# Rows of 64 KB instead of 32 KB for the loads and stores of a grouped instance norm

## Chip, cores, metric

The kernel runs on one core of a Trainium2 chip. The metric is the time of one execution on the device in microseconds (us), as a median of repeated runs. Runs over 1.5% above the fastest of the same kernel count as slow and are left out of ratios. Each kernel is compared with runs of the kernel before on the same chip in the same session.

## The reference, cut to what matters

```python
# x: (4, 8, 16, 256, 256) float32, gamma: (8, 16)
mu    = x.mean(axis=(3, 4), keepdims=True)          # over 65536 values of one channel
var   = ((x - mu) ** 2).mean(axis=(3, 4), keepdims=True)
out   = (x - mu) / np.sqrt(var + 1e-5) * gamma[None, :, :, None, None]
```

There are 512 channels of 256 KB each, so 134.2 MB come in and 134.2 MB go out. Nothing can be stored before its whole channel has been read.

## The kernel before

A unit is 16 channels of 65536 values. It lies on 128 partitions, each with an eighth of a channel: 8192 float32, one *row* of 32 KB. A unit moves as one DMA of 128 rows. Six slots take turns; slot `u % 6` is loaded, summed, normalised in place and stored, and then loaded again.

```python
    S = 8;  K = P // S;  F = HW // S        # 8 partitions a channel, rows of 8192 float32 = 32 KB
    U = n_ch // K                           # 32 units
    AHEAD = 6
    xv = x....rearrange("(u p f) -> u p f", p=P, f=F)
    slots = [data.tile([P, F], F32, name=f"xt{i}") for i in range(AHEAD)]
    def load(u, queue):
        queue.dma_start(out=slots[u % AHEAD][:], in_=xv[u])
    # ... first six loads, constants (cut) ...
    for u in range(U):
        t = slots[u % AHEAD]
        nc.vector.reduce_sum(out=st[:, u, 0:1], in_=t[:], axis=AX.X)                 # L103
        nc.scalar.activation(out=junk[:], in_=t[:], func=ACTF.Square, accum_out=st[:, u, 1:2])  # L104
        # ... matmul over the 8 partitions of a channel, 1/std, scale (cut) ...
        nc.vector.tensor_scalar(out=t[:], in0=t[:], scalar1=ps[:, 0:1], scalar2=scale[:, u:u+1],
                                op0=ALU.add, op1=ALU.mult)                           # L126
        nc.scalar.dma_start(out=ov[u], in_=t[:])                                     # L130
        if u + AHEAD < U:
            load(u + AHEAD, nc.sync)                                                 # L48
```

Loads go through the queue of SP (q1 in the profile), stores through that of ACT (q10). Both queues are served by the same 16 DMA engines.

## Time and profile before

| | before |
|---|---|
| median (range), 3 runs | 627.18 us (626.75 to 627.25) |
| span of the profiled run | 625.2 us |
| busiest compute engine | DVE, 71% |
| DMA slices at nine tenths or more | all but the first and the last |
| rate in the middle | 432 GB/s |
| last data of the 16 DMA engines | 622.8 to 623.6 us |

The last row comes from the trace's packet records: each row (a "packet" there) has a start and a duration. The records can be chained into 16 engines. The overlap matters below: from start to start a 32 KB row takes 1209.4 ns in the mean, not its recorded 1213. The records do not number the engines. The lines of the profile that show the bound are in the prediction. This is how the end looks, by windows (columns: window and its length, busy time and count of PE, PEld, DVE, ACT and POOL, the granted clock, the share of busy DMA engines, GB/s), for the kernel before:

```profile
600.00:620.00 20.00, 0.00 (x0) 0.00 (x0) 0.00 (x0) 0.00 (x0) 0.00 (x0) 1.00 1.00 431
620.00:623.00 3.00, 0.00 (x0) 0.00 (x0) 0.00 (x0) 0.00 (x0) 0.00 (x0) 1.00 0.81 350
623.00:626.00 3.00, 0.00 (x0) 0.00 (x0) 0.00 (x0) 0.00 (x0) 0.00 (x0) 1.00 0.00 0
```

The transfers run full to the end and stop at once: nothing follows in the third window.

### The profile page before, as it was taken

The numbers are of one execution on the slowest core, as the hardware profiler recorded it, in microseconds if no ns is written. First come the engines' busy times: TensorE is split into PE (matmuls) and PEld (weight loads), VectorE is DVE, ScalarE is ACT, GpSimd is POOL, SyncE is SP. The second block draws the span as 40 slices with busy tenths as digits, with TensorE's granted clock in tenths as the row PEclk, the third lists the DMA queues.
The fourth block names the chain that finished last, engine by engine and source line by source line (L and its number), as shares of the span: only waits on it lengthen the run. The fifth ranks groups of instructions, "written<-read, shape, count | busy, mean of one in ns | idle before, by whom it ended". The sixth has DMA issues, their size and how long they took to land.

```text
span 625.2 us, 626 instructions
## 1 busy us (share of the span) xinstructions
PE 21.4 (3%) x80; PEld 19.5 (3%) x80; DVE 443.2 (71%) x162; ACT 238.8 (38%) x98; POOL 1.3 (0%) x9
## 2 busy tenths in 40 slices
PE   2000000000000000000000000000000000000000
PEld 2000000000000000000000000000000000000000
DVE  0699999998867668676687766776667867668620
ACT  0444444444444224443244432344423443224400
POOL 0000000000000000000000000000000000000000
DMA  8999999999999999999999999999999999999998
GB/s 369 436 417 424 434 436 436 436 436 437 434 436 434 426 426 430 434 436 436 436 434 434 436 434 434 430 426 430 434 436 436 436 432 434 436 436 434 426 426 365
DMA packets 9220, 268.46 MB, mean 429 GB/s; under 512 B 1025, under 2 KB 1026, under 8 KB 1026
## 3 DMA queue, kind: packets, MB, share of 16 engines
q10 hardware_dynamic: 4898, 142.61, 52.8%
q1 hardware_dynamic: 4320, 125.83, 46.8%
q14 instruction: 2, 0.02, 0.0%
HBM read 134.22 MB, written 134.22 MB: 429 GB/s over the span
## 4 chain that ended last, share of the span: by engine, by line
another core or an unknown queue 64%; DMA 16%; DVE 13%; SPq 1%; PE 1%; issue 0%; ACT 0%
DMA xt<-in_x_dram 9%; DVE st L103 8%; DMA out_dram<-xt 7%; DVE xt L126 4%; SPq L48 1%; PE ps L112 1%; ACT std L117 0%; DVE nvar L113 0%; DVE rstd L121 0%; DVE scale L123 0%
## 5 line engine op out<-in xcount | busy, mean ns | idle before, releaser
L103 DVE TENSOR_REDUCE st<-xt 128x1 f32<-128x8192 f32 x32 | 277.9, 8684 | 111.2 <-DMA xt<-in_x_dram 111.2
L104 ACT ACTIVATE junk<-xt 128x8192 uint8<-128x8192 f32 x32 | 225.0, 7030 | 272.2 <-DMA xt<-in_x_dram 229.0
L126 DVE TENSOR_SCALAR xt<-xt,ps,scale 128x8192 f32<-128x8192 f32 x32 | 145.6, 4550 | 1.2
L117 ACT ACTIVATE std<-nvar,eps_t 128x1 f32<-128x1 f32 x32 | 9.4, 294 | 79.6 <-DVE nvar L113 79.6
L112 PE MATMUL ps<-st,navg 128*128 128x2 f32 x64 | 17.9, 349 | 568.0 <-DVE st L103 568.0
L112 PEld LDWEIGHTS ps<-st,navg 128*128 128x128 f32 x64 | 16.0, 312 | 569.8 <-issue 569.8
L113 DVE TENSOR_SCALAR nvar<-ps 128x1 f32<-128x1 f32 x32 | 9.2, 287 | 23.8 <-PE ps L112 23.8
L121 DVE RECIPROCAL rstd<-std 128x1 f32<-128x1 f32 x32 | 5.3, 164 | 11.6 <-ACT std L117 11.6
L104 ACT ACTIVATION_READ_ACCUMULATOR junk<-xt 128x1 f32 x32 | 6.0, 186 | 0.0
L123 DVE TENSOR_TENSOR scale<-rstd,g_col 128x1 f32<-128x1 f32 x32 | 5.1, 159 | 1.1
L84 PE MATMUL g_ps<-one,g_rep 1*128 1x1 f32 x16 | 3.5, 346 | 2.9 <-DVE g_rep L79 2.9
L84 PEld LDWEIGHTS g_ps<-one,g_rep 1*128 1x128 f32 x16 | 3.5, 325 | 2.9 <-POOL navg L68 2.9
L90 DVE COPY g_col<-g_ps 128x8 f32<-128x8 f32 x1 | 0.2, 166 | 3.7 <-PE g_ps L84 3.7
L74 ACT ACT_TABLE_LOAD x1 | 1.3, 1283 | 2.2 <-issue 2.2
L79 DVE COPY g_rep<-g_row 1x1024 f32<-1x1024 f32 x1 | 0.7, 681 | 2.1 <-DMA g_row<-in_gamma_dram 2.1
L64 POOL TENSOR_SCALAR_AFFINE_SELECT navg<-navg 128x128 f32<-128x128 f32 x1 | 0.4, 403 | 0.1
L68 POOL TENSOR_SCALAR_AFFINE_SELECT navg<-navg 128x128 f32<-128x128 f32 x1 | 0.4, 398 | 0.1
L63 POOL MEMSET navg<- 128x128 f32 x1 | 0.2, 220 | 0.0
L74 ACT ACTIVATE root_eps<-eps_t 128x1 f32<-128x1 f32 x1 | 0.2, 203 | 0.0
L147 POOL MEMSET const-bfloat16-1.0<- 128x1 bf16 x1 | 0.1, 101 | 0.0
L147 POOL MEMSET const-uint8-127<- 128x1 uint8 x1 | 0.1, 101 | 0.0
L147 POOL MEMSET const-float32-0.0<- 128x1 f32 x1 | 0.1, 98 | 0.3 <-issue 0.3
(3 smaller groups left out, 0.3 us busy)
## 6 DMA issues: line engine op xcount, KB each, us to landing
out_dram<-xt ACTq DMA_DIRECT2D x32, 4096.0 KB, 67.1
xt<-in_x_dram SPq DMA_DIRECT2D x30, 4096.0 KB, 33.8
xt<-in_x_dram ACTq DMA_DIRECT2D x2, 4096.0 KB, 33.3
g_row<-in_gamma_dram ACTq DMA_DIRECT2D x1, 0.5 KB
```

What stands on the lines that cost most here:

```text
L48: queue.dma_start(out=slots[u % AHEAD][:], in_=xv[u])
L74: nc.scalar.activation(out=root_eps[:], in_=eps_t[:], func=ACTF.Sqrt)
L79: nc.vector.tensor_copy(out=g_rep[:], in_=g_row[:].rearrange("o (n k) -> o n k", n=NG).unsqueeze(3).to_broadcast([1, NG, K, S]),)
L84: nc.tensor.matmul(out=g_ps[:, n : n + 1], lhsT=g_rep[:, n].rearrange("o k s -> o (k s)"), rhs=one[:], start=True, stop=True,)
L103: nc.vector.reduce_sum(out=st[:, u, 0:1], in_=t[:], axis=AX.X)
L104: square = nc.scalar.activation(out=junk[:], in_=t[:], func=ACTF.Square, accum_out=st[:, u, 1:2],)
L112: nc.tensor.matmul(out=ps[:], lhsT=navg_w, rhs=st[:, u], start=True, stop=True)
L113: nc.vector.tensor_scalar(out=nvar[:, u : u + 1], in0=ps[:, 0:1], scalar1=ps[:, 0:1], scalar2=ps[:, 1:2], op0=ALU.mult, op1=ALU.add,)
L117: nc.scalar.activation(out=std[:, u : u + 1], in_=nvar[:, u : u + 1], func=ACTF.Sqrt, bias=eps_t[:], scale=-1.0,)
L121: nc.vector.reciprocal(out=rstd[:, u : u + 1], in_=std[:, u : u + 1])
L123: nc.vector.tensor_mul(out=scale[:, u : u + 1], in0=rstd[:, u : u + 1], in1=g_col[:, g : g + 1],)
L126: nc.vector.tensor_scalar(out=t[:], in0=t[:], scalar1=ps[:, 0:1], scalar2=scale[:, u : u + 1], op0=ALU.add, op1=ALU.mult,)
```

## The change

The intent: a DMA-bound kernel with full queues can only be made shorter by moving fewer bytes or by spending less per row. A 32 KB row took 1213 ns, of which some 8 ns are not data by the prediction's estimate. With rows of 64 KB there are half as many. A unit becomes 32 channels on 128 partitions with a quarter of a channel each, three slots take the place of six, and two DMAs, each of every second partition, move a unit. So that the larger last unit does not leave the stores waiting for arithmetic, the third last unit is stored in 32 KB rows (its rows then take fewer turns of the engines from the last load), and the last unit's statistics are divided by columns between DVE and ACT and its result is stored in two column halves. The apply is divided between DVE and ACT in all units. The core of the diff (constants, matrices and the small chain are cut):

```diff
-    S = 8; K = P // S; F = HW // S; U = n_ch // K; AHEAD = 6
-    xv = x....rearrange("(u p f) -> u p f", p=P, f=F)
+    SL = 3; FW = HW // 4; FN = FW // 2; V = n_ch // 32; DV = 10240
+    xw = xf.rearrange("(v h r f) -> v h r f", h=2, r=P // 2, f=FW)
-    slots = [data.tile([P, F], F32, name=f"xt{i}") for i in range(AHEAD)]
+    slots = [data.tile([P, FW], F32, name=f"xt{i}") for i in range(SL)]
+    def load_slot(v):
+        t = slots[v % SL]
+        for h in range(2):
+            nc.sync.dma_start(out=t[h::2], in_=xw[v, h])
 ...
+    def sums_shared(v, t, ps):                      # the last unit only
+        for k in range(18):
+            nc.vector.bn_stats(out=bs[:, k], in_=t[:, k * 512 : (k + 1) * 512])
+        squared(v, t, 9216, FW, 1)                  # ACT: squares, then sums
+        squared(v, t, 9216, FW, 0, ACTF.Identity)
 ...
+        parts = [(0, FW)] if v < V - 1 else [(0, FN), (FN, FW)]
+        for a, b in parts:
+            m = a + DV * (b - a) // FW
+            nc.scalar.activation(out=t[:, m:b], in_=t[:, m:b], func=ACTF.Identity, bias=shift, scale=scale)
+            nc.vector.tensor_scalar(out=t[:, a:m], in0=t[:, a:m], scalar1=ps[:, 0:1], scalar2=scale, ...)
-        nc.scalar.dma_start(out=ov[u], in_=t[:])
+            for c, d in [(a, b)] if v != V - SL else [(0, FN), (FN, FW)]:
+                for h in range(2):
+                    nc.scalar.dma_start(out=ow[v, h, :, c:d], in_=t[h::2, c:d])
```

## The prediction

> **What bounds the kernel now.** I read the page first for engine shares, then the transfer view of the middle of the run, then the packet records of the trace, then the start and the end in order of time. The page:
>
> ```profile
> PE 21.4 (3%) x80; PEld 19.5 (3%) x80; DVE 443.2 (71%) x162; ACT 238.8 (38%) x98; POOL 1.3 (0%) x9
> ...
> DMA  8999999999999999999999999999999999999998
> ...
> HBM read 134.22 MB, written 134.22 MB: 429 GB/s over the span
> ...
> L103 DVE TENSOR_REDUCE st<-xt 128x1 f32<-128x8192 f32 x32 | 277.9, 8684 | 111.2 <-DMA xt<-in_x_dram 111.2
> L104 ACT ACTIVATE junk<-xt 128x8192 uint8<-128x8192 f32 x32 | 225.0, 7030 | 272.2 <-DMA xt<-in_x_dram 229.0
> L126 DVE TENSOR_SCALAR xt<-xt,ps,scale 128x8192 f32<-128x8192 f32 x32 | 145.6, 4550 | 1.2
> ```
>
> No compute engine is over 71%; the two busy ones wait for loads. The transfers are at nine tenths or more in every slice but the first and the last. The transfer view of the window from 150 to 538 us (20 units) is flatter still, and shows loads (q1) and stores (q10) sharing evenly:
>
> ```profile
> DMA packets 5762, 167.79 MB, mean 432 GB/s; under 512 B 640, under 2 KB 640, under 8 KB 640
> ...
> q10 hardware_dynamic: 2880, 83.89, 50.1%
> q1 hardware_dynamic: 2880, 83.89, 50.1%
> ```
>
> Each queue has 2880 packets for 20 transfers: 128 rows and 16 completion writes each. In the trace's packet records a 32 KB row takes 1213 ns (8036 of the 8192 rows exactly that) and a completion write 9 ns. One of the 16 DMA engines carries 8192/16 = 512 rows and 64 completion writes: 512 x 1.213 + 64 x 0.009 = 621.06 + 0.58 = 621.6 us. The first row starts 1.8 us into the span, the last ends at 623.6: 621.8 us. So the 16 engines are idle for some 0.1 us in all, and the span is a sum: 1.8 (start) + 621.6 (rows) + 0.1 + 1.6 (last completion and end) = 625.2. The measured median, 627.18, is 2.0 above the span.
>
> The end confirms it (timeline of the last unit):
>
> ```profile
> 582.87 7.03 ACT L104 ACTIVATE junk<-xt 128x8192 uint8<-128x8192 f32 x1 [9.34 <-DMA xt<-in_x_dram]
> 582.87 8.69 DVE L103 TENSOR_REDUCE st<-xt 128x1 f32<-128x8192 f32 x1 [4.36 <-DMA xt<-in_x_dram]
> ...
> 593.34 4.55 DVE L126 TENSOR_SCALAR xt<-xt,ps,scale 128x8192 f32<-128x8192 f32 x1
> 597.92 0.34 ACTq L130 DMA_DIRECT2D out_dram<-xt  x1
> ```
>
> The last store is issued at 597.9 and the program ends 27.3 us later, though 4.2 MB take 9.7 us at 432 GB/s: it queues behind other stores. The last unit's arithmetic is hidden.
>
> **What the skill says.** The Trainium skill, "DMA: Bandwidth & Descriptors", section "Where 436 GB/s comes from": 16 ports of 32 B at 850 MHz give 435.2 GB/s. At that rate 32 KB take one engine 1024 beats, 1204.7 ns; the trace has 1213, so about 8 ns a row are not data. The same page, "Why small descriptors are slow", gives a fixed overhead per packet of about 3 cycles, 3.5 ns by that clock; the trace shows more, and its 8 ns decide. Its section "Queues, rings and completion order" says an engine goes round its queues packet by packet; the equal 2880 and 2880 agree. "SBUF — State Buffer", section "Door 1: The DMA port swizzle", says bandwidth depends on how many of 16 ports the partitions reach, and its formula puts partitions 0 to 63 on half of them. Every x transfer of the kernel before has 128 partitions, so its trace cannot test that. It explains why the change takes every second partition rather than halves of the tile.
>
> **The change part by part.**
>
> *Rows of 64 KB.* 16 units of 8.4 MB instead of 32 of 4.2; three slots of 64 KB per partition instead of six of 32, so the same 25.2 MB on chip. Each unit moves as two DMAs of 64 rows. I estimate a 64 KB row from the trace: the 8 KB instruction fetches take at least 309 ns and the 32 KB rows 1213, a slope of 0.03678 ns per byte, so 1213 + 32768 x 0.03678 = 2418 ns, 8 less than two short rows.
>
> *Count per engine.* Loads: 8 long rows a unit x 16 = 128. Stores: 14 units x 8 = 112 long; the third last and the last unit 2 x 16 = 32 short. Rows: 240 x 2.418 + 32 x 1.213 = 580.3 + 38.8 = 619.1. DMAs: 32 loads and 36 stores, 68 x 0.009 = 0.6. Together 619.7, against 621.6 before: **1.9 us saved**, if the engines stay as full as they were.
>
> *Does a gap open?* I walk the queues at 432 GB/s (8.4 MB in 19.4 us alone, 38.7 beside the other direction). The first unit lands near 21 us. Its sum is 2 x 8.68 = 17.4, its two squares 2 x 7.03 + 0.2 = 14.3 beside it; the small chain is 1.8 now (29.0 to 30.8) and gains one small multiply, 2.1; the apply is split, 10240 columns on DVE (4.55 x 10/8 = 5.7) beside 6144 on ACT (7.03 x 6/8 = 5.3). Arithmetic: 25.2 us per unit, below the 38.7 of transfer. The first store starts near 47, when the opening 25.2 MB of loads, 58 us of transfer, still run. From then each slot goes round in 3 x 38.7 = 116 us: about 39 for a load, 25 for arithmetic, 39 for a store, 103. That leaves 13 us spare, less than before but positive, and it mostly sits in the store queue, which is 25 us deep when a unit's result is ready. The half-slot loads help: the first half is issued when the first half of the old store has landed, about 7 us before the load queue would run dry by my walk. If it does run dry, the stores take the whole rate and nothing is lost.
>
> *The end.* By the walk, store 13 (of 0 to 15) starts near 548 with 5.8 MB of the last load left. Its 32 KB rows take turns with 64 KB rows, so the load gets two thirds: 20 us instead of 27, landing near 568. Left to store then: 5.5 MB of unit 13 and 8.4 of unit 14, 32 us, to 600. The last unit's statistics: 18 bn_stats of 512 columns on DVE, at the sum's 1.06 ns per column about 10 us plus starts; two ACT passes over 7168 columns, 2 x (7.03 x 7/8 + 0.19) = 12.7, the longer. With matmuls and small chain 2.8, then a first half apply of 2.8, the first half store is issued near 586 to 588, over 10 us before the queue is empty. The second half is ready 3 us later. So the end stays a queue of stores, and these two parts are worth nothing by themselves: they keep the tail of the larger unit (25 us of arithmetic; without them the load would land near 575 with 2.6 + 8.4 = 11 MB, also 25 us, left to store) from opening a gap.
>
> *Off the path:* 16 small chains instead of 32, and on GpSimd seven more selects of 0.4 us and one multiply while the first load runs.
>
> Sum: 627.18 - 1.9 = 625.3; I add 0.2 for a small gap somewhere in the thinner slack: **625.5 us**.
>
> **Rivals.**
> 1. *Ports collide.* If the 64 alternate partitions are dealt so that two engines serve one port at the same time, transfers slow by tens of per cent (650 to 900 us). For it: nothing in the trace tests the shape. Against: taking h, h+2, ... reaches every port, and a deal by partition gives each engine four rows on its own port, as the full tile has 1213 for nearly every row. I give it 4%.
> 2. *A gap through thinner slack:* coarser units leave 13 us where the six slots had more. A missed turn would show as idle transfers of 3 to 10 us: 628 to 635. Against: while any queue holds rows the engines are full, and both do in my walk.
> 3. *The gain does not exist:* a 64 KB row costs two 32 KB rows (2426 ns, or a split descriptor), and the time stays at 627.2. Or memory dislikes 64 KB strides by 1%: 633. The 8 ns surplus rests on a line through two lengths, of which the short ones are instruction fetches.
> 4. *A large gain:* even rows with no overhead at all take 512 x 1.2047 = 616.8 us, 4.3 less than now, so the floor is about 622.9. Faster by over 2% (below 614.6) would break the rate of the ports.
>
> **Range and chances.** The floor is 622.9 and no gain is 627.2; the lower end lies between floor and estimate, the upper leaves room for a gap or a slower row of a few us: 624.0 to 629.0. Faster by over 2%: 0.01. Slower by over 2% (rival 1 or a repeated gap): 0.05. Within: 0.94.
>
> **What would show it.** Right: 64 KB rows of about 2418 ns in the packet records; the same mid-run window at 433 GB/s instead of 432; half the packets per byte; no slice but the first and the last under nine tenths; the last store issued at 586 to 592 with over 20 us of stores behind it. Wrong: rows far above 2426 ns (ports or memory), dips in the transfer slices after each unit (slack), the last store issued when the store queue is already empty, or a chain at the end that runs through the last unit's statistics.

## The result, and the profile after

| | before | after |
|---|---|---|
| median of 6 runs (range), us | 627.05 (626.75 to 627.38) | 634.83 (632.51 to 636.72) |
| ratio after / before | | 1.0122 (95%: 1.0096 to 1.0148) |
| span of the profiled run, us | 625.2 | 634.8 |
| median 64 KB row, loads and stores alike, ns | | 2418 |
| mean load row, ns | 1218.6 | 2448.3 |
| last data, first and last of 16 engines, us | 622.8, 623.6 | 623.0, 633.2 |

Ratios here and below are the mean time of one kernel's fast runs over that of the other's of the same rounds, so they are not quite the ratio of the medians. The change is slower by 1.2% with an interval well above 1, and 634.83 lies outside the predicted range of 624.0 to 629.0. The prediction was wrong.

The page of the kernel after, lines that answer to those in the prediction:

```profile
PE 24.5 (4%) x102; PEld 23.1 (4%) x102; DVE 371.7 (59%) x122; ACT 320.9 (51%) x99; POOL 4.7 (1%) x17
...
DMA  9999999999999999999999999999999999999993
...
HBM read 134.22 MB, written 134.22 MB: 423 GB/s over the span
...
L123 DVE TENSOR_REDUCE st<-xt 128x1 f32<-128x16384 f32 x15 | 258.3, 17219 | 188.8 <-DMA xt<-in_x_dram 188.8
L114 ACT ACTIVATE junk<-xt 128x8192 uint8<-128x8192 f32 (+1 forms) x32 | 223.2, 6976 | 200.5 <-DMA xt<-in_x_dram 197.3
...
L168 DVE TENSOR_SCALAR xt<-xt,ps,cf 128x10240 f32<-128x10240 f32 (+1 forms) x17 | 89.9, 5296 | 0.0
```

DVE went from 71% to 59%, ACT from 38% to 51%: the apply was divided, as meant, and neither bounds anything. The rate over the span fell from 429 to 423 GB/s. The transfer slices read 9 everywhere, except the last: 3 instead of 8. The loss looks as if it sat at the end. The middle, the window from 150 to 538 us of the transfer view, seems untouched:

```profile
DMA packets 3200, 167.79 MB, mean 432 GB/s; under 512 B 638, under 2 KB 638, under 8 KB 638
...
q10 hardware_dynamic: 1607, 84.48, 50.3%
q1 hardware_dynamic: 1591, 83.30, 49.8%
```

The same 167.79 MB at the same 432 GB/s, with 3200 packets instead of 5762. A first suspicion is then the last unit's arithmetic, which the timeline of the kernel after shows:

```profile
582.87 6.18 ACT L114 ACTIVATE junk<-xt 128x7168 uint8<-128x7168 f32 x1 [7.51 <-DMA xt<-in_x_dram]
582.88 10.78 DVE L134 BATCH_NORM_STATS2 bs<-xt 128x6 f32<-128x512 f32 x18 [7.60 <-DMA xt<-in_x_dram]
...
600.33 1.74 ACTq L176 DMA_DIRECT2D out_dram<-xt  x2
...
605.10 1.77 ACTq L176 DMA_DIRECT2D out_dram<-xt  x2
```

The columns are start and duration in us, engine, line, operation with its tiles, count, and in brackets the idle time before with what ended it. The first half is stored from 600.33 us on, the second from 605.10. By the packet records some 3.5 us of older stores were still left at 600.33, and the last unit's 8.4 MB need 19.4 us at 432 GB/s: 600.3 + 3.5 + 19.4 = 623.2, which is where most engines end. So the stores did not come too late, though the spare was thin. The windows at the end show what happened instead (columns as above), for the kernel after:

```profile
600.00:620.00 20.00, 0.00 (x0) 0.00 (x0) 3.04 (x2) 3.25 (x2) 0.00 (x0) 1.00 0.97 418
620.00:623.00 3.00, 0.00 (x0) 0.00 (x0) 0.00 (x0) 0.00 (x0) 0.00 (x0) 1.00 0.91 393
623.00:626.00 3.00, 0.00 (x0) 0.00 (x0) 0.00 (x0) 0.00 (x0) 0.00 (x0) 1.00 0.28 120
626.00:629.00 3.00, 0.00 (x0) 0.00 (x0) 0.00 (x0) 0.00 (x0) 0.00 (x0) 1.00 0.10 44
629.00:632.00 3.00, 0.00 (x0) 0.00 (x0) 0.00 (x0) 0.00 (x0) 0.00 (x0) 1.00 0.08 33
632.00:636.00 4.00, 0.00 (x0) 0.00 (x0) 0.00 (x0) 0.00 (x0) 0.00 (x0) 1.00 0.03 12
```

The share falls in steps: 0.28, then 0.10, 0.08 and 0.03. One engine of 16 is 0.06. From 626 us on, one or two engines work on alone. The packet records give the last data of each engine, in order:

```
before  622.8 622.8 622.9 622.9 622.9 622.9 622.9 623.0 623.0 623.0 623.0 623.1 623.2 623.5 623.6 623.6
after   623.0 623.1 623.1 623.1 623.1 623.2 623.2 623.2 623.3 623.8 624.8 624.9 625.1 626.2 630.5 633.2
```

Ten engines of the kernel after finish at 623.0 to 623.8 us; one needs until 633.2. Every engine carries 272 rows, and none is idle for more than 0.3 us between 3 and 620 us, so the last one was slow while it worked. Summed over an engine, what its rows took beyond 2418 ns (or 1213 for short ones) is 2.3 to 2.6 us for most: 1.7 to 2.0 in the opening before 60 us, most of the rest after 500 (in the kernel before, 0.9 to 1.8 in all). On the last engine it is 12.1, on the second last 9.6. The last engine gathered 6.2 of its 12.1 us between 100 and 300 us, one row at a time. Here are its rows beside those of an engine that stayed in step (L load, S store, start in us + duration in us, from the packet records of the kernel after):

```
in step   S74.0+2.42 S76.4+2.42 L78.9+2.42 S81.3+2.42 L83.7+2.42 L86.1+2.42 S88.5+2.42 L90.9+2.42 S93.4+2.42
late      S74.6+2.42 S77.0+2.42 L79.4+2.59 S82.0+2.42 L84.4+2.42 L86.8+2.42 S89.3+2.42 L91.7+2.65 S94.3+2.42
```

So in this run the loss is not at the end: it is made in the middle, by single load rows that take 2.5 to 3.5 us instead of 2.42, 60 of the 63 between 90 and 500 us on six engines. There it does not show in any average, because the engine is busy all the same and the mean of 16 hardly moves.

The records also show a point that the prediction had otherwise. The opening's loads were used up at about 70 us; the next load was issued at 73.7 us and its rows began at 77.9. There the load queue was dry. From then on each load DMA mostly ended 4.8 us before the next one's rows began: two store rows in between, as at 74.0 and 76.4 above. The expectations below take this gap for a dry queue, but it is none by itself. The kernel before has the same gap of two store rows (2.4 us, 383 times between 60 and 520 us), though each of its loads was issued at least 12 us before the load ahead of it was done. What tells is the time of issue. In the kernel after, loads were issued from 3.1 us before to 0.7 us after the middle engine had done the load ahead (the first after the opening 4.4 us after, the last 2.9): the queue was nearly empty there. On whichever engine was the latest they were, after that first one, 3.9 to 7.1 us ahead: it was not the late engines that waited for loads.

### The profile page after: what moved, and what is told of

The parts are those of the page before. It is cut to its first block, busy times and chain, and to the rows that moved or that the text cites. A ratio compares the mean times of both kernels' runs of the same rounds, so it can differ in the third digit from the quotient of the medians.

```text
span 634.8 us, 667 instructions
## 1 busy us (share of the span) xinstructions
PE 24.5 (4%) x102; PEld 23.1 (4%) x102; DVE 371.7 (59%) x122; ACT 320.9 (51%) x99; POOL 4.7 (1%) x17
## 4 chain that ended last, share of the span: by engine, by line
DMA 59%; DVE 14%; another core or an unknown queue 12%; ACT 8%; PE 1%; issue 0%; SPq 0%; ACTq 0%; DVEq 0%
DMA out_dram<-xt 34%; DMA xt<-in_x_dram 25%; DVE st L123 14%; ACT xt L165 5%; ACT junk L114 2%; PE ps L126 0%; SPq L55 0%; ACTq L176 0%; PE ps L128 0%; PE ps L127 0%; ACT cf L157 0%; DVE cf L153 0%; DVE cf L158 0%; DVE cf L159 0%
## 5 line engine op out<-in xcount | busy, mean ns | idle before, releaser
L123 DVE TENSOR_REDUCE st<-xt 128x1 f32<-128x16384 f32 x15 | 258.3, 17219 | 188.8 <-DMA xt<-in_x_dram 188.8
L114 ACT ACTIVATE junk<-xt 128x8192 uint8<-128x8192 f32 (+1 forms) x32 | 223.2, 6976 | 200.5 <-DMA xt<-in_x_dram 197.3
L165 ACT ACTIVATE xt<-xt,cf 128x6144 f32<-128x6144 f32 (+1 forms) x17 | 88.5, 5207 | 12.6 <-DVE cf L160 10.8
L168 DVE TENSOR_SCALAR xt<-xt,ps,cf 128x10240 f32<-128x10240 f32 (+1 forms) x17 | 89.9, 5296 | 0.0
L157 ACT ACTIVATE cf<-cf,eps_t 128x1 f32<-128x1 f32 x16 | 4.7, 294 | 69.7 <-DVE cf L153 69.7
L126 PE MATMUL ps<-st,navg 128*128 128x1 f32 x30 | 8.8, 361 | 542.7 <-DVE st L123 542.7
L126 PEld LDWEIGHTS ps<-st,navg 128*128 128x128 f32 x30 | 7.5, 311 | 543.9 <-DVE st L123 507.5
L153 DVE TENSOR_SCALAR cf<-ps 128x1 f32<-128x1 f32 x16 | 4.6, 287 | 24.5 <-PE ps L128 23.1
L134 DVE BATCH_NORM_STATS2 bs<-xt 128x6 f32<-128x512 f32 x18 | 10.8, 677 | 7.6 <-DMA xt<-in_x_dram 7.6
L128 PE MATMUL ps<-st,navg 128*128 128x1 f32 x30 | 8.5, 352 | 0.0
L127 PE MATMUL ps<-st,navg 128*128 128x1 f32 x30 | 8.5, 352 | 0.0
L127 PEld LDWEIGHTS ps<-st,navg 128*128 128x128 f32 x30 | 8.2, 333 | 0.0
L128 PEld LDWEIGHTS ps<-st,navg 128*128 128x128 f32 x30 | 8.2, 333 | 0.0
L158 DVE RECIPROCAL cf<-cf 128x1 f32<-128x1 f32 x16 | 2.6, 164 | 5.8 <-ACT cf L157 5.8
```

Of the source, the lines that this page charges most:

```text
L114: sq = nc.scalar.activation(out=junk[:, : b - a], in_=t[:, a:b], func=func, accum_out=st[:, v, col : col + 1],)
L123: nc.vector.reduce_sum(out=st[:, v, 0:1], in_=t[:], axis=AX.X)
L126: nc.tensor.matmul(out=ps[:, 0:1], lhsT=navg_w, rhs=st[:, v, 0:1], start=True, stop=True)
L127: nc.tensor.matmul(out=ps[:, 1:2], lhsT=navg_w, rhs=st[:, v, 1:2], start=True, stop=False)
L128: nc.tensor.matmul(out=ps[:, 1:2], lhsT=navg_w, rhs=st[:, v, 2:3], start=False, stop=True)
L134: nc.vector.bn_stats(out=bs[:, k], in_=t[:, k * BW : (k + 1) * BW])
```

## The experiments

"Late" below means a row over 60 ns beyond 2418 (or 1213) that started between 90 and 500 us. The questions, in order: is it the empty load queue, the row length, the shape with every second partition, the arithmetic, or the two parts at the end? All diffs are against the kernel after unless said otherwise.

### 1. The kernel after again

No edit.

> The changed kernel once more, as the control of this call. Theory 1 (the load queue runs out before each half slot's load is issued; the first row after that is slow on the engine that is already last; the end waits for that engine) and theory 2 (rows of 64 KB are slow on some engines by themselves) both expect what was seen: 632 to 637 us, most engines done near 623 us of the span and one or two 7 to 10 us later, a gap of 4.8 us between the load rows of one DMA and the next on every engine.

Median 631.92 us (629.7 to 635.27), ratio 1.0080 (1.0046 to 1.0115), in a new session. The profiled run, 629.7, was the best of its four; 26 of 1350 load rows were late and no store row, and the engines ended at 622.3 to 624.0 but one, at 626.4. The gap of 4.8 us before each load was there too, with loads issued 1.4 to 2.1 us ahead of the middle engine's need after the first. The loss is real, but its size differs from run to run by some 7 us over the two sessions. Whatever is to be told apart has to be larger than that, or be seen in the records.

### 2. A fuller load queue by short rows in one unit

```diff
-            nc.sync.dma_start(out=t[h::2], in_=xw[v, h])
+            for c, d in [(0, FW)] if v != SL - 1 else [(0, FN), (FN, FW)]:
+                nc.sync.dma_start(out=t[h::2, c:d], in_=xw[v, h, :, c:d])
```

Loads of the third unit in 32 KB rows take half the turns beside the first stores, so that the load queue should last longer.

> One edit: the loads of the third unit (the last of the three opening ones) in rows of 32 KB. While they share with the first store of 64 KB rows, the store gets two thirds, so the first half of slot 0 is free before the opening loads are out of the queue, and the loads keep that lead. All other rows stay 64 KB. Theory 1: no gap between load DMAs (0 to 2.4 us in place of 4.8), no slow first rows, engines finish within 1 to 2 us of each other, 624.5 to 627 us. Theory 2: as the control, 632 to 637, as 252 of 256 rows an engine are as long as before.

Median 708.55 us (707.89 to 710.76), ratio 1.1304: the expectation was missed by 80 us. The page of this kernel has dips all through (transfer slices):

```profile
DMA  9999999999999899797997988979989799896974
GB/s 407 422 412 414 427 433 407 418 444 407 433 337 430 337 377 437 263 437 314 366 444 274 403 351 314 429 285 407 407 311 455 318 400 425 309 435 281 470 340 174
```

In the records three engines took their first store row 1.2 us before the other 13 (53.0 to 53.5 against 54.5 to 55.0). From 67 us on most long rows of these three, first stores and from 83 us loads too, took 2.5 to 3.9 us, while the 13 mostly stayed at 2.42:

```
in step     S69.4+2.42 ... S73.0+2.42 ... S76.6+2.42
out of step S68.0+2.92 ... S72.2+3.29 ... S76.7+3.10
```

352 of 1165 load rows and 140 of 1218 store rows were late. The dips fit the other engines waiting for the three: the store whose rows ended at 158.9 us on the middle engine ended at 176.4 on the last, and the load that took its place was issued at 177.0. It did not test the load queue, but it showed stretched rows with a loss ten times as large, in a kernel that put two row lengths side by side for one unit.

### 3. Short rows, three slots, all 128 partitions

```diff
-            nc.sync.dma_start(out=t[h::2], in_=xw[v, h])
+            nc.sync.dma_start(out=t[:, h * FN : (h + 1) * FN], in_=xw[v, :, h * FN : (h + 1) * FN])
-                for h in range(2):
-                    nc.scalar.dma_start(out=ow[v, h, :, c:d], in_=t[h::2, c:d])
+            for c in range(a, b, FN):
+                nc.scalar.dma_start(out=ow[v, :, c : c + FN], in_=t[:, c : c + FN])
```

with the views as `(v p f)`, and the averaging matrix and the gamma column rewritten for four neighbouring partitions a channel. Everything else as after: three slots, both parts at the end, the divided apply.

> The same three slots of 64 KB, the same units, arithmetic and number of DMAs, but every load and store is a half of the columns of all 128 partitions: rows of 32 KB everywhere. Theory 1: the slots turn over as in the control, so the load queue still runs out (gaps of about 2.4 us, two rows), first rows are still slow on the last engine: 629 to 634 us with engines 3 to 8 us apart. Theory 2: no long rows, so as the kernel before, 626.5 to 628, engines within 1 us.

Median 629.02 us (628.45 to 629.72), ratio 1.0030 (1.0015 to 1.0045). 6 of 2705 load rows were late and the engines ended at 623.4 to 625.3. The gap before a load was two store rows here too, 2.4 us; by the times of issue the load queue was dry once, by 2.4 us near 70 us, and then at least 4 us ahead. Midway the engines were up to 8 us apart, and yet hardly any rows stretched. So with 32 KB rows neither three large slots nor engines out of step cost more than 2 us. What is left between this kernel and the one after is row length and partitions, which runs 5 and 6 separate.

### 4. Four slots in the kernel before

```diff
-    AHEAD = 6
+    AHEAD = 4
```

(against the kernel before)

> The kernel before with four slots of 32 KB rows in place of six: less lead for the loads, nothing else. Theory 1: the load queue runs out between DMAs and some engines fall behind: 628 to 634 us. Theory 2: rows of 32 KB, so as before, 627 to 628 us.

Median 629.09 us (628.86 to 629.76), ratio 1.0034. The load queue was dry once, when a load was issued at 52.8 us that was wanted at 38; after that loads were issued 4.6 to 6.4 us ahead instead of 12. 2 of 2719 load rows were late. The 2 us that it lost are at the end, where the timeline shows the last load's sum and the last store:

```profile
599.86 8.69 DVE L103 TENSOR_REDUCE st<-xt 128x1 f32<-128x8192 f32 x1 [4.36 <-DMA xt<-in_x_dram]
...
614.91 0.34 ACTq L130 DMA_DIRECT2D out_dram<-xt  x1
```

With fewer slots the last load lands at 599.9 instead of 582.9, the last store is issued at 614.9, and the other stores had ended shortly before it. So a load queue that ran empty once, for 15 us, cost no stretched rows; the store queue that ran empty at the end left the engines idle for 0.7 to 1.7 us.

### 5. Every second partition, rows of 32 KB

```diff
-    slots = [data.tile([P, FW], F32, name=f"xt{i}") for i in range(SL)]
+    slots = [data.tile([P, 2, FN + 32], F32, name=f"xt{i}") for i in range(SL)]
-            nc.sync.dma_start(out=t[h::2], in_=xw[v, h])
+            nc.sync.dma_start(out=t[h::2, :, 0:FN], in_=xw[v, h].rearrange("r (c f) -> r c f", c=2))
```

The tile has a gap of 128 bytes in the middle, so that the same DMA of every second partition must take two rows of 32 KB for each of 64 KB; stores likewise. The apply is divided 8192 to 8192.

> Alternate partitions as in the changed kernel, but each 64 KB row moved as two rows of 32 KB (the tile has a gap of 128 B between its two column halves, so that the rows can't be joined); the split of the scaling is 8192 columns each. With the run of 32 KB rows over all 128 partitions this makes a square of shape against row length. Theory 2 (long rows are what is slow): as that run, 627 to 629.5 us, no slow rows after the opening 90 us. Theory 3 (a transfer of every second partition makes DMA engines get in each other's way as soon as they are out of step, which is how three engines had rows of 3 us in the run with a lead for the loads): slow rows after the opening, some engines 3 us and more behind at the end, 629 to 645 us.

Median 628.43 us (628.24 to 628.62), ratio 1.0024 (1.0009 to 1.0038); 2 of 2711 load rows late, engines end at 623.2 to 624.7, although late in the run they were over 10 us apart at the same row. The windows at the end (columns as above):

```profile
620.00:623.00 3.00, 0.00 (x0) 0.00 (x0) 0.00 (x0) 0.00 (x0) 0.00 (x0) 1.00 0.94 404
623.00:626.00 3.00, 0.00 (x0) 0.00 (x0) 0.00 (x0) 0.00 (x0) 0.00 (x0) 1.00 0.05 22
```

The trailing steps of the kernel after are gone.

### 6. All 128 partitions, rows of 64 KB

```diff
-        for h in range(2):
-            nc.sync.dma_start(out=t[h::2], in_=xw[v, h])
+        nc.sync.dma_start(out=t[:], in_=xw[v])
-                for h in range(2):
-                    nc.scalar.dma_start(out=ow[v, h, :, c:d], in_=t[h::2, c:d])
+                nc.scalar.dma_start(out=ow[v, :, c:d], in_=t[:, c:d])
```

> Rows of 64 KB, all 128 partitions in one transfer: one load and one store a unit in place of two each; third last and last unit as in the changed kernel. Theory 3: every 64 KB row after the opening takes 2418 ns, engines finish within 1.5 us of each other, 624.5 to 627.5 us, so faster than both. Theory 2: slow rows and stragglers as in the changed kernel, 629 to 636 us. If the full slot turn is too coarse (a new load waits for the whole store): gaps in the transfers, over 630 us without slow rows.

Median 629.98 us (629.6 to 631.1), ratio 1.0046 (1.0029 to 1.0063); 69 of 1352 load rows late. Eight engines end at 622.4 to 622.8, the others at 624.4 to 627.8:

```profile
620.00:623.00 3.00, 0.00 (x0) 0.00 (x0) 0.00 (x0) 0.00 (x0) 0.00 (x0) 1.00 0.89 382
623.00:626.00 3.00, 0.00 (x0) 0.00 (x0) 0.00 (x0) 0.00 (x0) 0.00 (x0) 1.00 0.25 109
626.00:629.00 3.00, 0.00 (x0) 0.00 (x0) 0.00 (x0) 0.00 (x0) 0.00 (x0) 1.00 0.03 11
```

Runs 3, 5, 6 and the kernel after are a square of two row lengths by two shapes. Late load rows: 6 and 2 of some 2700 with short rows, 69 and 63 of some 1355 with long ones (26 in the repeat), whichever the partitions. With one length in both directions, the length decides whether rows stretch. The times agree: runs 5 and 6 were made on one chip in one session, and the slowest with short rows took 628.62 us, the fastest with long ones 629.6; for runs 3 and 1, again of one session, the medians are 629.02 and 631.92. Between the shapes the times are not so clean: 630.0 against 631.9 to 634.8 with long rows, from different chips and sessions.

### 7. The same without the two parts at the end

As run 6, with `sums(v, t, ps)`, `parts = [(0, FW)]` and `[(a, b)]` for all units.

> The run before without both tail parts: third last unit stored in 64 KB rows, last unit's statistics and store as in all units. The prediction's walk has the last store ready about when the store queue runs out: 0 to 6 us above the run before. If the two parts are worth nothing, the same within 0.5 us.

Median 640.67 us (639.96 to 642.63), ratio 1.0224: 10.7 us above run 6. The timeline shows why:

```profile
577.98 0.34 ACTq L169 DMA_DIRECT2D out_dram<-xt  x1
...
591.63 17.22 DVE L117 TENSOR_REDUCE st<-xt 128x1 f32<-128x16384 f32 x1 [13.76 <-DMA xt<-in_x_dram]
...
617.21 0.34 ACTq L169 DMA_DIRECT2D out_dram<-xt  x1
```

The last load lands at 591.6, its store is issued at 617.2, and the stores of the unit before were done by about 603 on 11 engines (608 on the last): most engines were idle for some 15 us. In this shape the two parts are worth ten microseconds, not nothing. 40 of 1357 load rows were late here, but the pause let all engines catch up: they ended at 637.4 to 637.6.

### 8. Neighbouring halves of the partitions

```diff
-            nc.sync.dma_start(out=t[h::2], in_=xw[v, h])
+            nc.sync.dma_start(out=t[64 * h : 64 * h + 64], in_=xw[v, 64 * h : 64 * h + 64])
```

and stores likewise.

> A measurement of the disputed cost, not a candidate: each unit moved as partitions 0 to 63 and 64 to 127, 64 KB rows. If the ports of the tile's memory are what engines share (theory 3), 64 neighbouring partitions reach half of them and rows take up to twice 2418 ns: 900 to 1250 us, less where both halves are in flight together. If ports play no part: 625 to 637 us.

One look: 894.04 us (a single run, so its state is unknown). A load row took 4013 ns in the mean. The opening, in which nearly only loads run, is the cleanest place to compare. This kernel, window 5 to 45 us:

```profile
5.00:45.00 40.00, 0.00 (x0) 0.00 (x0) 0.83 (x1) 0.84 (x1) 0.00 (x0) 1.00 1.01 210
```

The kernel after, same window:

```profile
5.00:45.00 40.00, 1.41 (x6) 1.35 (x6) 19.70 (x6) 16.16 (x6) 0.93 (x2) 1.00 1.03 446
```

210 against 446 GB/s with a busy share of 1.0 in both (a row counts where it starts, so a short window can show a few per cent too much): the engines are busy all the time and move half. That is what the Trainium skill's port formula ("SBUF — State Buffer", "Door 1: The DMA port swizzle") gives for partitions 0 to 63, half of the ports, and it is why the change takes every second partition. It has nothing to do with the loss of the kernel after, whose rows take 2418 ns.

### 9. Short loads beside long stores

As run 6, with the loads of run 3 (two column halves of 32 KB).

> Three slots, loads as two column halves of 128 partitions (32 KB rows), stores as whole units in 64 KB rows. So far: long rows were slow only in loads, never in stores, and mostly on an engine that is out of step with the others. Theory 2 narrowed (long load rows, out of step, are what is slow): no slow rows after the opening although stores are long, engines within 1.5 us of each other; one engine's work 256 x 1.213 + 112 x 2.418 + 32 x 1.213 + 0.6 = 620.8, so 626 to 628 us. If long rows of either direction do it: 629 to 634.

Runs of 678.37, 677.76, 674.67 and 655.49 us, median 676.22. By the 1.5% rule three of the four, the profiled one among them, count as slow, and there is no ratio. The granted clock was 1.0 in each and the kernel before ran in 626.83 to 627.08 beside them, so the spread is this kernel's own; only its trace is used here, and its fastest run is 28 us above the kernel before. The expectation that this would cure it was missed. Transfer slices:

```profile
DMA  8999999999999999999699999989999997999538
```

165 of 2568 load rows and 182 of 1266 store rows were late. Here long *store* rows stretched, and short load rows beside them too. In this run long stores beside short loads were worse than long rows in both directions.

### 10. Long loads beside short stores

As run 6, with the stores of run 3.

> The mirror: loads as whole units in 64 KB rows, stores as column halves of 32 KB rows, all 128 partitions. Theory 2 narrowed: slow load rows after the opening (some per cent of them over 60 ns late), engines several us apart at the end, 628.5 to 634 us. If both directions have to be long: 626.5 to 628.5.

Median 627.34 us (626.76 to 628.07), ratio 1.0006 (0.9991 to 1.0021). 40 of 1376 load rows were late, but spread over the engines, which ended at 622.4 to 623.6. Here the load queue was truly dry: after the opening each load was issued some 8 us after the middle engine had done the load ahead (the first 17 us), and its rows mostly began some 12 us after. So an empty load queue costs nothing here, and so do late rows that are few and spread: no engine's rows took more than 2.9 us beyond the median in all. And mixed lengths are not always bad: here, with the short rows in the stores, nothing was lost. This is as fast as the kernel before and not faster.

### 11. The transfers of the kernel after alone

The loop body cut to the stores and the next load: no sums, no apply. Its output is wrong, which doesn't matter for the time.

> Wrong on purpose: the changed kernel's transfers alone, each half slot stored as soon as it has landed, no arithmetic (out is x). The first store starts at about 13 us in place of 49, so the opening loads are still in the queue for long when slots come free and the load queue should not run out. Theory 1 (long rows are slow only after the load queue has run out): no slow rows, engines within 1.5 us, 624.5 to 626 us. Theory 2 (long load rows that are out of step are slow, full queue or not): slow rows and stragglers again if engines fall out of step, 628 to 640 us; if they stay in step, as theory 1.

630.2, 630.26, 630.54 and once 684.21 us: fast runs' ratio 1.0053 (1.0036 to 1.0070). 170 of 1352 load rows late, ends at 625.1 to 627.1. The gap of two store rows before each load was 4.8 us as before, but the load queue was full: after the opening each load was issued 25 to 56 us before the load ahead of it was done. The pages show it in the median time from a load's issue to its landing, the last number of each line, for the kernel after:

```profile
xt<-in_x_dram SPq DMA_DIRECT2D x32, 29.1
```

and for this run:

```profile
xt<-in_x_dram SPq DMA_DIRECT2D x32, 77.5
```

So the empty load queue is cleared, and arithmetic too: without either the long rows still stretch. And the loss is of another kind. Each engine had 8 to 12 late rows and took 4.5 to 6.0 us beyond the median in all: no engine falls behind, all are slower.

### 12. The transfers of the kernel before alone

The same cut in the kernel before.

> The same of the kernel before: its transfers alone, 32 KB rows, no arithmetic (out is x). Both theories: the transfers are the bound there, so 626.5 to 627.5 us, as with the arithmetic; engines within 1 us.

Median 626.47 us (626.41 to 626.66), ratio 0.9992; 0 of 2720 load rows late, ends at 622.8 to 623.5, with the same gap of 2.4 us before every load although each was issued over 12 us ahead. This is the floor that the transfers of the kernel before have, and that kernel is 0.6 us above it: it had hardly anything left to give. And with run 11 it makes the same comparison as the square, with nothing but transfers in the kernel.

### 13. Transfers alone, trying again for a full load queue

As run 11, without the gamma load and the constants.

> Wrong on purpose (out is x): the changed kernel's transfers alone, and without the load of gamma, so that the six opening loads are issued early and stores start at 13 us beside them; several loads stay queued. The check that the setting works: no gap between the load rows of one DMA and the next beyond the single store row that alternates (2.4 us). Theory 1 (the queue must run dry): no slow rows after the opening, 624 to 626 us. Theory 2 with step (long load rows out of step): if the engines take the first store at two different rows, slow rows and 628 us or more in spite of the full queue; if all take it at the same row, 624 to 626.

Median 631.25 us (630.4 to 635.97), ratio 1.0083; 123 late load rows, ends at 623.9 to 628.3. The expectation's check was the gap, and the gap was still 4.8 us; but, as shown above, the gap does not tell a dry queue. By the times of issue (31.26 us for rows that began at 89.5, 50.66 for rows at 109.2, and so on) the queue never emptied in this run, and long rows stretched: its theory 1 falls.

### 14 to 16. Transfers alone, first store delayed by 400, 1100 and 1800 columns of work

```diff
+        if v == 0:
+            nc.scalar.activation(out=t[0:1, 0:400], in_=t[0:1, 0:400], func=ACTF.Identity)
```

(1100 and 1800 in the others.) The thought: if all 16 engines meet the first store at the same row, none gets out of step.

> Transfers alone as before (out is x), the first store delayed by rewriting 400 elements of one partition on the activation engine (about 0.5 us). Without delay 9 and 7 engines took the first store one row apart, and it ran 630.2 to 630.5 (once 684). If being out of step is the cause: where all 16 engines take the first store at the same row, no slow rows after the opening and 624 to 626 us; where they divide, slow rows and over 628. If it is a consequence only: slow rows in either case. Of the three delays (0.5, 1.1, 1.7 us; a row is 2.4) at least one should leave them in step.

> As h2 with 1100 elements (about 1.1 us): the same rule, by what the trace shows of the engines' first store row.

> As h2 with 1800 elements (about 1.7 us): the same rule, by what the trace shows of the engines' first store row.

| | runs, us | late loads, stores in the profiled run |
|---|---|---|
| 400 | 637.47, 645.05, 693.41, 710.05 | 99, 17 |
| 1100 | 669.94, 633.75, 644.79, 662.83 | 231, 184 |
| 1800 | 636.38, 633.41, 635.34, 668.18 | 91, 11 |

All at clock 1.0, yet up to 11% apart within one kernel; six of the twelve count as slow by the 1.5% rule, the profiled one of 1100 among them. The fast runs alone give ratios of 1.0227 (1.0157 to 1.0297, unclear) for 400 and 1.0117 (1.0097 to 1.0137) for 1800, so there is little to compare in the times beyond "not better, and often much worse than run 11". In all three profiled runs the 16 engines did take their first store at the same row (20.7 to 21.5 us), and the stretched rows came all the same, at first mostly on the engines that were latest within that step, 0.4 to 0.7 us behind the first. In the run with 1800 columns one engine had rows of 2.49 to 2.85 us from 38 us on. The theory that an engine has to be a whole row out of step falls: being late by a fraction of a row was followed by stretched rows.

### 17. The third last unit in 64 KB rows

```diff
-            for c, d in [(a, b)] if v != V - SL else [(0, FN), (FN, FW)]:
+            for c, d in [(a, b)]:
```

> The changed kernel with its third last unit stored in 64 KB rows like the others. The last load then gets half instead of two thirds of the rate beside that store, and lands some 5 us later (588 instead of 583), the first half store some 5 us later too: 1 to 3 us past the point where the store queue is empty. Expect 2 to 4 us over the control: 634 to 639 us, transfers idle for 1 to 4 us near 604 us of the span. If the 3.5 us to spare suffice: 630 to 637 as the control.

Median 634.07 us (632.3 to 634.84), ratio 1.0108 (1.0091 to 1.0124). The first half of the last unit was stored later than in the kernel after, by 2.9 us:

```profile
603.18 1.75 ACTq L176 DMA_DIRECT2D out_dram<-xt  x2
```

yet the engines had no real pause around it (share 0.93 to 0.97), and the time is within the spread of the kernel after. Its engines ended at 626.4 to 628.8, with 293 of 1345 load rows late, spread over all engines (15 to 24 on each). The loss here is even: every engine took 5.3 to 7.9 us beyond the median, the mean load row was 2470.5 ns, and the rate from 150 to 538 us was 430 GB/s against 433 in run 1. So a straggler is one way to lose the time, and many late rows on all engines another.

### 18. The last unit like the others

```diff
-        (sums if v < V - 1 else sums_shared)(v, t, ps)
+        sums(v, t, ps)
-        parts = [(0, FW)] if v < V - 1 else [(0, FN), (FN, FW)]
+        parts = [(0, FW)]
```

> The changed kernel with the last unit treated like the others (sum on DVE, squares on ACT, one apply, one store of 64 KB rows), third last unit still stored in 32 KB rows. Arithmetic 25 us after the last load lands near 583: store issued near 608, 4 us after the queue is empty, and it starts 2 us later. Expect 5 to 8 us over the control: 637 to 642 us, transfers idle for about 6 us near 605 us of the span.

Median 630.7 us (629.13 to 635.96), ratio 1.0070 (1.0014 to 1.0126): none of the loss that was expected. The last load happened to land earlier in the profiled run than in the kernel after, and the store was issued in time:

```profile
577.01 17.22 DVE L123 TENSOR_REDUCE st<-xt 128x1 f32<-128x16384 f32 x1 [6.75 <-DMA xt<-in_x_dram]
...
602.59 1.80 ACTq L176 DMA_DIRECT2D out_dram<-xt  x2
```

194 of 1351 load rows were late, again on all engines (7 to 17 each), which ended at 625.6 to 628.5. Either part can be left out without a loss beyond the spread; run 7, which leaves out both, shows that they are not worthless together, though it has the other shape.

### What the records of several runs say together

Rows that started between 95 and 560 us, load rows only, parted by how many of the other engines were loading at the same time (mean over the row's duration); the share that was late:

| | fewer than 11 others | 11 or more |
|---|---|---|
| after | 56 of 520 | 15 of 1013 |
| run 6, whole, 64 KB | 88 of 631 | 4 of 919 |
| run 1, after again | 27 of 1142 | 1 of 409 |
| run 3, 32 KB | 6 of 2264 | |
| run 5, 32 KB | 2 of 1346 | |

A long load row was late in one of nine cases in the kernel after while the others were storing or mixed, and in one of 68 when nearly all were loading too. Each engine takes four rows of a load DMA; of those started between 60 and 600 us in the kernel after, 56 of 416 first rows were late, which come after the gap of two stores, and 5, 26 and 18 of the second, third and fourth (416, 432, 432); of 1736 long store rows, 4. But these are the runs that show it, and others with the same rows do not. In run 18, 174 of 1153 load rows were late with fewer than 11 others loading and 60 of 383 with 11 or more, the same share; in run 17 it is 283 of 1222 and 53 of 313. Nor is it always the first row: in run 11 it was the third (171 of 448, against 25 first rows), in run 17 the fourth (232 of 432, against 78). So neither the gap nor what the others do is shown to be the reason; no run proves a mechanism.

## Why the prediction was wrong, point by point

*The row of 64 KB: right in its duration, too large in its saving.* 2418 ns were predicted from a line through two lengths, and 2418 is the median of loads and of stores. Packets per byte fell by almost half. The saving was smaller than it said, though. It multiplied recorded durations, and these overlap by 3 to 4 ns a row. From start to start two short rows take 2 x 1209.4 = 2418.8 ns and a long one 2414.1 (without a completion write between): 4.7 ns saved for each long row, not 8, so 240 x 4.7 = 1.1 us an engine, not 1.9. The close agreement of its 621.6 with the measured 621.8 was partly luck: it left out 0.9 to 1.8 us by which some rows of each engine exceed 1213 ns, and counted the overlaps, 512 x 3.6 = 1.8 us. (Its 1204.7 ns for the data alone is an estimate from the page's rate; against 1209.4 some 5 ns are left, not 8.) And the typical engine after lost about 1.0 us by its slower rows, 2.4 against 1.4 us, half of it after 500 us. So ten engines finished at 623.0 to 623.8, where in the kernel before all end at 622.8 to 623.6; nothing was left even there. In run 1 the first ten ended at 622.3 to 622.8, up to half a microsecond earlier.

*The sum: the failed step.* The prediction says "Together 619.7, against 621.6 before: **1.9 us saved**, if the engines stay as full as they were", and backs the condition with "If it does run dry, the stores take the whole rate and nothing is lost". The engines did stay full. What failed is that all rows were given the same duration and the 16 engines were treated as one pipe. The term missing from the sum is what the rows of the *last* engine take beyond 2418 ns: 12.1 us, where the typical engine has 2.4. The difference, 9.7 us, is about the 9.6 us between the last data of the two profiled runs (633.2 and 623.6). Had this run's excess been even, it would have cost less: the mean load row is 30 ns over 2418, which for 128 load rows an engine is 3.9 us, 1.5 more than the typical engine has anyway. Runs 11, 17 and 18 are such cases with more late rows: 4.2 to 7.9 us on every engine, and ratios of 1.0053 to 1.0108. Either way the step that failed is the duration: with long rows in both directions not every row takes the median.

*The walk of the queues: wrong in itself, and not the cause.* It had the first half-slot load issued 7 us before the load queue ran dry. The queue was dry at about 70 us, and the next load was issued at 73.7. But runs 3 and 4, with short rows, ran dry once too, by 2.4 and 15 us, with 6 and 2 late rows, and run 10 ran dry before nearly every load and lost nothing; in runs 11 and 13 the queue stayed full, and 170 and 123 load rows were late. So the clause "If it does run dry ... nothing is lost" is not the step that failed.

*The end: landed, with less room than said.* First half store near 586 to 588 predicted, issued at 600.33; last load 568 predicted, landed 582.87. The walk gave the last load two thirds of the rate and too early a start. The spare of "over 10 us" was about 3.5. The statement that the two parts are worth nothing by themselves but keep a gap from opening is half confirmed: each alone could go (runs 17, 18), and without both the gap opened (run 7, 10.7 us), in the other shape. The parenthesis that without them the load would land near 575 was wrong: 591.6 there.

*Rival 1, ports:* not in this shape (2418 ns). Run 8 shows that the rival was real for neighbouring halves, 210 against 446 GB/s.

*Rival 2, a gap:* its time, 628 to 635, includes the result, but its sign, idle transfers, is missing: no slice fell below nine tenths before the last. It would have been right by luck.

*Rival 3, "memory dislikes 64 KB strides by 1%: 633":* the nearest. It had every row slower, and the median row is exact. What the runs show is single long rows stretched by 0.1 to 1.1 us, on few engines or, as in run 17, on all, where the mean load row is 2% longer. Chance and range: 624.0 to 629.0 allowed for a slower mean, not for one engine of 16, and 0.94 was too sure of it.

*What stays open.* Why some long rows stretch, and short ones beside short ones hardly ever; and what decides how many there are and on how many engines, which makes 629.7 or 636.7 of the same program. A load queue that never empties does not prevent it (runs 11 and 13). No version was found that beats the kernel before; its transfers alone take 626.47.

## What to carry to other kernels

A kernel bound by transfers ends with the last of its 16 DMA engines, and neither the mean rate nor the busy slices show that one is falling behind: look at the last data of each engine, or at whether the transfer share falls in steps of a sixteenth at the end. Where all are slowed alike, as in run 17, the mean rate does show it (430 against 433 GB/s). Work out what a longer row can save from start to start, not from recorded durations, before building on it: here it was 4.7 ns of 2419, 0.2% of the time, and rows that took longer than the median took it back several times over. A gap between two DMAs of one queue is not an empty queue: compare the time of issue with the end of the DMA ahead. Do not change row lengths in one direction alone without a run, since a long row beside short ones cost from nothing (run 10) to 13% (run 2).

## What the Trainium skill lacked or had wrong

- "DMA: Bandwidth & Descriptors", "Rules for kernel authors", recommends 128 partitions and at least 1 MiB per DMA for the highest bandwidth, and "Perfetto Trace Analysis", "What “DMA-bound” means", says that large descriptors are what matters. Neither says that there is a point beyond which larger rows lose: 64 KB rows in both directions gave ratios of 1.0046 to 1.0122 with all arithmetic and both parts at the end in place, 32 KB rows in the same shapes 1.0024 and 1.0030.
- No page has rows of one length that stretch singly, so that engines with equal work end unevenly (what is said there of slower DMA engines has other reasons): 622.8 to 623.6 us before, 623.0 to 633.2 after.
- No error was found in "DMA: Bandwidth & Descriptors", "Why small descriptors are slow", against what the prediction says. It has a fixed overhead of about 3 cycles a packet, by an estimate at the fabric's clock 3.5 ns. From start to start two 32 KB rows take 2418.8 ns and one of 64 KB 2414.1, 4.7 ns apart, which is near it; the prediction's 8 ns came from durations that overlap.
- The same page's rules on two transfers to disjoint partition halves say not to bother, because they share the engines anyway. What neighbouring halves cost (210 against 446 GB/s in the opening, 894 us in all) follows from the port formula cited in run 8. What the pages lack is that two transfers of every second partition keep the full rate: 446 GB/s in the opening of the kernel after.
